# Block transposes on VectorE in the second pass's heads, an earlier K-times-values product, and reordered opening loads in a gated pooling and HGRN2 layer

## The chip, the cores and the metric

The kernel runs on one core of one Trainium2 chip. The metric is the device time of one execution in microseconds (us). A core has five engines that matter here, each with its own in-order queue: PE (TensorE: matrix products into the PSUM memory; a weight load, PEld, goes ahead of each product), DVE (VectorE), ACT (ScalarE), POOL (GpSimd) and SP (SyncE, which issues most DMAs). They meet through semaphores only.

## The reference, cut to what matters

One layer over a sequence of 2048 tokens with 1024 channels, all in float32:

```python
ada = c_act @ w_ada + b_ada                      # shift, scale, gate
h = rms_norm(x, g_pre) * (1 + scale) + shift
pv, pg, hq, hf, hi, hg, mg_pool, mg_hgrn = split(h @ w_in)
branch_a = (pool(pv) * silu(pg)) @ w_pool_o
f = lb + (1 - lb) * sigmoid(hf); k = 1 - f; q = silu(hq); v = hi
S_t = diag(f_t) S_{t-1} + k_t v_t^T;  o_t = S_t^T q_t       # per head, 8 heads of 128
branch_b = (rms_norm(o) * silu(hg)) @ w_hgrn_o
merged = sigmoid(mg_pool) * branch_a + sigmoid(mg_hgrn) * branch_b
x = x + gate * rms_norm(merged @ w_out, g_post)
```

The recurrence is computed by chunks: within a chunk the scores q times decayed k are formed and applied to v, and between chunks a 128x128 state per head is carried on.

## The kernel before, in words

Tokens are worked on in two passes (p = 0 and 1) of 1024, each in two halves (t = 0 and 1) of 512 = 4 chunks of 128. Every large product is a float32 product written as three (high and low parts, `three`, L355) and most of them are saved one in eight by a seven-product scheme (`quad`, L621). A pass has these stages: the values `V` (`v_job`, `rows7`), eight heads, the pooling projection (`a_job`), the branch-B projection (`b_fast`), and the output projection (`y_fast`).

A head h is three `quad`s: `fq` (forget gate and query), `m` (the merge gates) and `gp` (the pool part and the HGRN output gate). The last head takes `gp` before `m`. A `quad` is seven groups of 12 products of 128x512 (`pa`, `pb`, `pe` are its PSUM tiles), and after the second and each later group it calls `tick()`. A tick lets every active generator `hgrn(p, h, t)` (L676) go on to its next `yield`. Two generators (t = 0 and 1) start after each `fq`; one more tick stands after each `quad`. So a head is 21 ticks, and a generator, at about 30 yields, runs over into the next head.

What a generator does, in order: the gate F, K = 1 - F and the query Q; a tree of decay products `TT`; then scores at rising distances. For each distance it runs 16 small PE products K by Q-variants (`X`) into the PSUM tile `psa` (`scores`), DVE copies them under a mask into `PT` (`put`, L726 and L732, `COPY_PREDICATED`), and DVE multiplies K and Q by decay (`kup`, `qup`, all through L498). Five yields (`GAP`) lie between two distances. The last scores (distances 32 and 64, L801 to L807) go to `PT` by ACT (L808 to L810). After them:

- L811 and L812: `kup(32)` and `kup(64)` finish K; two yields later PE turns K's four 128x128 chunks into PSUM (`pk`, helper `turn`, L353), and ACT copies it to `KS` (L820);
- two yields later `pd` = KS times values on PE; DVE carries the state over the four chunks (`SC`, L830), starting from the tile S[h];
- three yields later `po` = PT times values plus Q times state on PE, and ACT copies the last state back to S[h] (L839);
- ACT squares and sums `po` (L843), POOL makes the norm's factor `ss`, two yields later ACT scales into `on` (L850), and two yields later PE turns `on` into PSUM (`pot`, L353); DVE multiplies it with the gate: `sgg` (L857).

In the second pass's heads every PE instruction is tied to the one written before it (`line`, `mm` L348, `turn`), so PE runs in the order of the program text. The other engines' order is set by the framework's scheduler, which places each instruction when it reckons its inputs to be there; `issue_after` (`after(...)`) adds a tie by hand.

The pool part of an even head makes window sums on DVE: `W<-PV`, `W<-W` and `pm`, with window 2 in head 0, 4 in head 2, 8 in head 4 and 16 in head 6. In an odd head it is a gate (`spg`) and needs less.

The second pass's values come from `rows7`, whose first result copies are ACT's `A.copy(vt, src)` (L1389). Weights are split into high and low part by ACT and DVE (`item_split`, `split`, L181).

The opening (first pass): SP issues `ident`, eight loads of small parameter rows (L133), eight loads of x (L515), then `w_ada` and the first weights (L384, L185). PE turns the rows (`pst`), then x (`xT`, L536), multiplies `w_ada` (L399), turns the sum (L407), and starts the values (`psV`).

Of the kernel before, what the change touches and what calls it, by code (L numbers as in the profile page):

```python
# [8 lines left out]
F32 = mybir.dt.float32  # L9
# [22 lines left out]
O_PV, O_PG, O_Q, O_F, O_I, O_G, O_MP, O_MH = 0, 512, 1024, 2048, 3072, 4096, 5120, 6144  # L32
# [36 lines left out]


@with_exitstack
def tile_block(ctx: ExitStack, tc: tile.TileContext, x, c, w_ada, b_ada, g_pre, g_post, w_in,
               pool_w, pool_scale, lb_logits, hgrn_norm_g, w_pool_o, w_hgrn_o, w_out,
               ident_d, mask_d, icnt_d, w_pv_t, x_t, w_quad, w_po, out):
    nc = tc.nc
    V, A, G, PE, SP = nc.vector, nc.scalar, nc.gpsimd, nc.tensor, nc.sync
    x, out = x[0], out[0]
    w_ada, w_in = w_ada[0], w_in[0]
# [14 lines left out]
    def utile(name, dt=F32):  # L93
        return up.tile([P, T], dt, tag="u", name=name)
# [4 lines left out]
    def after(ins):  # L99
        return tc.issue_after(ins.ins) if ins is not None else nullcontext()  # L100

    last = {"st": None, "whl": None}

    state = {"prep": 0, "use": 0, "pre": 0}

# [16 lines left out]


    ident = cst.tile([P, P], F32, name="ident")
    SP.dma_start(ident, ident_d)
    rows = utile("rows")[0:48, 0:P]
    G.memset(rows, 0.0)
    r0 = 0
    idx = {}
    for nm, src, n in (("c", c[0:1, :], 8), ("bsh", b_ada[0:1, 0:D], 8), ("bsc", b_ada[0:1, D:2 * D], 8),  # L130
                       ("gpre", g_pre[0:1, :], 8), ("lb", lb_logits[0:1, :], 8),
                       ("psc", pool_scale[0:1, :], 4), ("ng", hgrn_norm_g[0:1, :], 1)):
        SP.dma_start(rows[r0:r0 + n, :], src.rearrange("o (r k) -> (o r) k", k=P))  # L133
        idx[nm] = (r0, r0 + n)
        r0 += n
    mask = cst.tile([P, MASK_W], U8, name="mask")
# [2 lines left out]
    def const_setup():  # L139
        for o in range(0, MASK_W, T):  # L140
            w = min(T, MASK_W - o)
            mi = utile(f"mask_i{o}", I32)
            SP.dma_start(mi[:, 0:w], mask_d[:, o:o + w])
            G.tensor_copy(mask[:, o:o + w], mi[:, 0:w])
        SP.dma_start(icnt, icnt_d)

    pst = px.tile([P, T], F32, tag="px", name="pst")
    PE.transpose(pst[:, 0:48], rows, ident[0:48, 0:48])
# [31 lines left out]
    def split(src32, hi, lo, e=None):  # L180
        return A.copy(hi, src32), (e or V).tensor_tensor(lo, src32, hi.bitcast(F32), op=SUB)  # L181
# [8 lines left out]

    def item_split(name, raw):
        w = item_tile(name)
        split(raw, w[:, 0:T], w[:, T:2 * T])
        return w

    def keep(key, w, again):
# [154 lines left out]
    def turn(o, i):  # L351
        with after(line["it"] if line["on"] else None):
            line["it"] = PE.transpose(o, i, ident)  # L353
# [137 lines left out]
    def v2(ap, n):  # L491
        return ap.rearrange("p (a b) -> p a b", b=n)

    def bc(ap, n):
        return ap.unsqueeze(2).broadcast_to([P, ap.shape[1], n])

    def tt(o, a, b, op=MUL, e=None):
        return (e or V).tensor_tensor(o, a, b, op=op)  # L498
# [13 lines left out]
    def x_rows(tok, load):  # L512
        xs = [utile(f"x{tok}_{n}") for n in range(2)]
        for n in range(2):
            load(xs[n], x[tok * P:(tok + 1) * P, n * T:(n + 1) * T])  # L515
        return xs

    def x_first(cx, xss):
# [14 lines left out]
        return it, ic  # L533

    def x_turn(xss, k, tk, pt_):
        PE.transpose(pt_[:, tk * P:(tk + 1) * P], xss[tk][k // 4][:, (k % 4) * P:(k % 4 + 1) * P], ident)  # L536

    def x_turned(cx, k, pt_, on_act):
        h32 = cx["h32"][0, k] = utile(f"h32_0_0_{k}")
# [136 lines left out]
    def hgrn(p, h, t, cx):  # L676
# [104 lines left out]
        for hh in (2, 8):  # L781
            scores(X)
            put(blk(ptf, NB, hh), s48[:, :, 0:16])
            put(blk(ptf, NB, 2 * hh), s48[:, :, 16:32])
            put(blk(ptf, NB, 2 * hh), s48[:, :, 32:48])
            kup(hh)
            kup(2 * hh)
            if hh == 2:
                X = build(8, NB, 16)
            else:  # L790
                X = qp.tile([P, T], F32, tag="qr", name=f"X32_{n}")
                x32 = X[:, 0:T // 2].rearrange("p (b w) -> p b w", w=32)
                A.copy(x32, blk(Q, NB // 2, 32))
                qup(32)
                x64 = X[:, T // 2:T].rearrange("p (b w) -> p b w", w=64)
                tq = Tb[32].rearrange("p (a b) -> p a b", b=4)
                q64 = blk(Q, NT, 64)
                tt(x64, q64, bc(tq[:, :, 1], 64))
            for _ in range(GAP):
                yield  # L800
        s64 = s48  # L801
        for cc in range(NT):
# [5 lines left out]
        A.copy(pt[0:64, :, 64:128], s64[0:64, :, 32:96])  # L808
        A.copy(pt[0:32, :, 32:64], s64[0:32, :, 0:32])
        A.copy(pt[64:96, :, 96:128], s64[64:96, :, 0:32])  # L810
        kup(32)  # L811
        kup(64)  # L812
        tt(q64, x64, bc(tq[:, :, 0], 64))
        yield
        yield
        pk = px.tile([P, T], F32, tag="px", name="pk" + n)
        for cc in range(NT):
            turn(pk[:, cc * P:(cc + 1) * P], K[:, cc * P:(cc + 1) * P])
        KS = utile("KS" + n)
        A.copy(KS, pk)  # L820
        yield
        yield
        pd = px.tile([P, NT, P], F32, tag="px", name="pd" + n)
        for cc in range(NT):
            mm(pd[:, cc, :], KS[:, cc * P:(cc + 1) * P], vv(cc), True, True)
        SC = utile("SC" + n)
        sts = [S[h]]
        for cc in range(NT):
            nxt = SC[:, cc * P:(cc + 1) * P]
            V.scalar_tensor_tensor(nxt, sts[-1], Tb[128][:, cc:cc + 1], pd[:, cc, :], op0=MUL, op1=ADD)  # L830
            sts.append(nxt)
        yield
        yield
        yield
        po = px.tile([P, NT, P], F32, tag="px", name="po" + n)
        for cc in range(NT):
            mm(po[:, cc, :], pt[:, cc, :], vv(cc), True, False)
            mm(po[:, cc, :], Q[:, cc * P:(cc + 1) * P], sts[cc], False, True)
        A.copy(S[h], sts[NT])  # L839
        ss = sp.tile([P, NT], F32, tag="ss", name="ss" + n)  # L840
        for cc in range(NT):
            junk = sp.tile([P, T], BF16, tag="jx", name=f"junk{cc}_{n}", bufs=1)
# [5 lines left out]
        on = utile("on" + n)  # L848
        for cc in range(NT):
            A.activation(on[:, cc * P:(cc + 1) * P], po[:, cc, :], AF.Copy, scale=ss[:, cc:cc + 1])  # L850
        yield
        yield
        pot = px.tile([P, T], F32, tag="px", name="pot" + n)
        for cc in range(NT):
            turn(pot[:, cc * P:(cc + 1) * P], on[:, cc * P:(cc + 1) * P])
        og = cx["G"].pop((h, t))
        V.scalar_tensor_tensor(og, pot, col("ng"), og, op0=MUL, op1=MUL)  # L857
        two_out("G", p, h, t, og, cx, h == NH - 1)
# [369 lines left out]
    def krow(src, k, o):  # L1228
        return src[k * P:(k + 1) * P, o:o + T]
# [77 lines left out]
    for q in range(4):  # L1307
        parts[q] = ada_load(q)
        for k in (2 * q, 2 * q + 1)[:7 - 2 * q]:
            early["v", 0, k] = raw_load(f"e{k}", (krow(w_in, k, O_I), None))  # L1310
    xs1 = [x_rows(NT + tk, SP.dma_start) for tk in range(NT)]
    behind = {}
    ix, ic = x_first(cxs[0], xss)
    it = ada_mul(0)
    with after(ix), after(ic):
        prep()
    with after(it), after(ix):
# [46 lines left out]
    for p in range(NPASS):  # L1364
# [19 lines left out]
        if p > 0 and FAST_V:  # L1384
            def v_got(n, t, tk, src):
                vt = src
                if t == 0:
                    vt = utile(f"V{p}_{t}_{n}_{tk}")
                    A.copy(vt, src)  # L1389
# [12 lines left out]
            rows7(f"V{p}", cx["mv"], v_got, v_step)  # L1402
# [185 lines left out]
```

## Time and profile before

| | before |
|---|---|
| median of 3 runs | 1736.92 us (1736.89 to 1737.13) |
| the profiled execution | 1735.28 us |
| its span from first to last instruction | 1733.5 us |
| PE busy | 1708.2 us, 99% |
| DVE busy | 1219.8 us, 70% |
| ACT busy | 855.6 us, 49% |
| granted PE clock | 0.998 |

The 1.8 us between the profiled execution and its span lie outside of the first and last instruction. All sums are made against this one execution; the median lies 1.64 us above it, so a difference worked out in the trace is taken off the median. In a timeline a row gives start, length, engine, line, operation, output and inputs, a count, and in brackets how long the engine sat idle before, and who released it. Lengths overlap: the next instruction of an engine can begin before the one in front has ended, so the step from one start to the next is what an instruction costs in a queue.

### The profile page before, as it was taken

What the parts mean: (1) busy time and instruction counts of PE and PEld (TensorE: products, weight loads), DVE (VectorE), ACT (ScalarE), POOL (GpSimd) and SP (SyncE); (2) the same over time, 40 slices, a digit from 0 to 9 for tenths busy, and PEclk for the clock granted to TensorE, in tenths of its full rate; (3) what the DMA queues carried; (4) which work ended last, traced back from release to release, by engine and by line L of the source; (5) the groups of instructions that cost most, each with busy time, mean ns of one, the idle gap of its engine ahead of it and who ended that gap; (6) DMA issues with size and microseconds to landing.
All of it is one profiled execution on the core that took longest, in us unless ns stands there. A gap on an engine that the chain in (4) does not pass through costs nothing.

```text
span 1733.5 us, 31740 instructions
## 1 busy us (share of the span) xinstructions
PE 1708.2 (99%) x11805; PEld 1405.6 (81%) x11805; DVE 1219.8 (70%) x2546; ACT 855.6 (49%) x1975; POOL 95.9 (6%) x152
## 2 busy tenths in 40 slices
PE   7999999999999999999999999999999999999998
PEld 4788888888888887888887888888888888888886
DVE  4668888888988889788787264455455545766666
ACT  4746656566565655342755334344343343534243
POOL 1100000100000000100030000000000000000002
PEclk9999999999999999999999999999999999999999
DMA  9759887888789788976795765665665656564657
GB/s 310 270 171 331 285 305 281 294 289 324 268 290 330 265 291 283 352 252 226 268 312 173 251 203 183 203 206 173 218 194 172 218 179 193 183 231 168 210 195 265
DMA packets 191288, 425.33 MB, mean 245 GB/s; under 512 B 19311, under 2 KB 44572, under 8 KB 191134
## 3 DMA queue, kind: packets, MB, share of 16 engines
q1 hardware_dynamic: 181918, 406.52, 68.9%
q10 hardware_dynamic: 9216, 16.78, 2.7%
q8 instruction: 93, 1.52, 0.4%
q14 instruction: 61, 0.50, 0.1%
HBM read 267.51 MB, written 155.71 MB: 244 GB/s over the span
## 4 chain that ended last, share of the span: by engine, by line
PE 93%; DVE 2%; DMA 2%; ACT 2%; issue 1%; SPq 1%; POOL 0%; DVEq 0%; POOLq 0%; ACTq 0%
PE pam L348 10%; PE pagp L348 10%; PE pafq L348 10%; PE pem L348 5%; PE psA L348 5%; PE pefq L348 5%; PE psV L348 5%; PE pegp L348 5%; PE raB L348 4%; PE ray L348 4%; PE psa L348 4%; PE po L348 3%; PE pbfq L348 2%; PE pbm L348 2%; PE pbgp L348 2%; PE raV L348 2%
## 5 line engine op out<-in xcount | busy, mean ns | idle before, releaser
L181 DVE TENSOR_TENSOR whl<-wr,whl 128x512 fp32r<-128x512 f32 x160 | 108.9, 686 | 37.6 <-ACT whl L181 36.9
L181 ACT CAST whl<-wr 128x512 fp32r<-128x512 f32 x160 | 99.4, 624 | 69.1 <-issue 15.4
L348 PE MATMUL pagp<-hT,whl 128*128 128x512 f32 x384 | 128.1, 394 | 0.4 <-ACT c12gp L634 0.4
L348 PE MATMUL pam<-hT,whl 128*128 128x512 f32 x384 | 128.2, 394 | 0.2
L348 PE MATMUL pafq<-hT,whl 128*128 128x512 f32 x384 | 126.3, 390 | 0.0
L181 ACT CAST whl<-wri 128x512 fp32r<-128x512 f32 x76 | 47.1, 622 | 117.9 <-PE psA L348 27.8
L732 DVE COPY_PREDICATED PT<-mask,psa 128x256 f32<-128x256 uint8 x160 | 86.1, 547 | 11.9 <-PE psa L348 11.9
L348 PEld LDWEIGHTS pagp<-hT,whl 128*128 128x128 f32 x384 | 72.1, 188 | 16.2 <-ACT c12gp L634 0.5
L348 PEld LDWEIGHTS pam<-hT,whl 128*128 128x128 f32 x384 | 72.1, 188 | 15.4 <-ACT c12m L634 0.6
L348 PEld LDWEIGHTS pafq<-hT,whl 128*128 128x128 f32 x384 | 72.1, 188 | 15.2 <-ACT c12fq L634 0.2
L348 PE MATMUL psA<-Ph,whl 128*128 128x512 f32 x256 | 82.5, 395 | 0.4 <-ACT Ph L181 0.4
L348 PE MATMUL psV<-whl,hB 128*128 128x512 f32 x256 | 80.8, 400 | 1.6 <-ACT hB L1324 1.1
L498 DVE TENSOR_TENSOR K<-K,TT 128x256 f32<-128x256 f32 x192 | 80.6, 425 | 0.0
L348 PE MATMUL pagp<-lT,whl 128*128 128x512 f32 x192 | 74.9, 390 | 0.0
L348 PE MATMUL pam<-lT,whl 128*128 128x512 f32 x192 | 74.8, 390 | 0.0
L348 PE MATMUL pafq<-lT,whl 128*128 128x512 f32 x192 | 74.7, 389 | 0.0
L181 DVE TENSOR_TENSOR whl<-wri,whl 128x512 fp32r<-128x512 f32 x76 | 51.8, 685 | 26.1 <-ACT whl L181 25.4
L726 DVE COPY_PREDICATED PT<-mask,psa 128x256 f32<-128x256 uint8 (+1 forms) x96 | 52.1, 543 | 21.7 <-PE psa L348 21.7
L348 PEld LDWEIGHTS psa<-X,K 128*32 128x32 f32 x2816 | 48.5, 110 | 19.4 <-issue 17.1
L857 DVE SCALAR_TENSOR_TENSOR sgg<-pot,vec,sgg 128x512 f32<-128x512 f32 x32 | 23.1, 746 | 56.0 <-PE pot L353 56.0
L680 DVE TENSOR_SCALAR F<-F 128x512 f32<-128x512 f32 x16 | 6.8, 426 | 77.3 <-ACT F L679 77.2
L348 PEld LDWEIGHTS psV<-whl,hB 128*128 128x128 f32 x256 | 48.2, 191 | 14.6 <-ACT hB L181 1.7
(569 smaller groups left out, 4789.6 us busy)
## 6 DMA issues: line engine op xcount, KB each, us to landing
wr<-in_w_quad_dram SPq DMA_DIRECT2D x88, 256.0 KB, 4.0
whl<-scr_y SPq DMA_DIRECT2D x36, 512.0 KB, 3.5
sm<-Sd SPq DMA_DIRECT2D x64, 256.0 KB, 5.4
whl<-scr_b SPq DMA_DIRECT2D x32, 512.0 KB, 3.3
scr_y<-rfy SPq DMA_DIRECT2D x40, 256.0 KB, 3.1
x<-in_x_dram SPq DMA_DIRECT2D x32, 256.0 KB, 5.7
wa<-in_w_ada_dram SPq DMA_DIRECT2D x32, 256.0 KB, 6.2
V<-Vd SPq DMA_DIRECT2D x16, 512.0 KB
```

What stands on the lines that cost most here:

```text
L181: return A.copy(hi, src32), (e or V).tensor_tensor(lo, src32, hi.bitcast(F32), op=SUB)
L348: line["it"] = PE.matmul(o, lhsT=l, rhs=r, start=start, stop=stop, skip_group_check=True)
L498: return (e or V).tensor_tensor(o, a, b, op=op)
L680: V.tensor_scalar(F, F, 1e-30, None, op0=MAX)
L726: V.copy_predicated(dst.rearrange("p (c a) b -> p c a b", c=NT), m.unsqueeze(1).broadcast_to(shp), src.unsqueeze(2).broadcast_to(shp))
L732: V.copy_predicated(dst.rearrange("p (c q) a b -> p c q a b", c=NT), m, src.rearrange("p c (a b) -> p c a b", b=b).unsqueeze(2) .broadcast ...
L857: V.scalar_tensor_tensor(og, pot, col("ng"), og, op0=MUL, op1=MUL)
```

## The change

In the second pass's heads (`if p`), three things:

- K is no longer turned by PE. As soon as the second-to-last distance is done, DVE writes a decayed copy `KD` with three multiplications, and turns it into `KS` with `block_turn`: sixteen `V.transpose` instructions a generator, each over four 32x32 blocks (32 partitions x 128 elements), four in each of four ticks. The finishing `kup(32)` and `kup(64)`, PE's `pk` and ACT's copy to `KS` go, and `pd` comes right behind the last scores. Seven yields then lie ahead of `po`, where before there were two, two and three.
- The outputs `on` are turned in the same way, in the tile `ot` in SBUF, four ticks long (two in the last head), and PE's `pot` goes. The gate product reads `ot`.
- The state is handed on in `SC` (`carry`), in both passes; S[h] is copied once, at the end of pass 0.

Besides: the eight small loads become one (`rows`, packed and padded ahead of the kernel), `ident` is loaded from ACT's queue, the first `w_ada` product is tied behind the last turn of x, and in `item_split` ACT's copy of a weight is tied behind the last copy of the second pass's values (`last["act"]`).

```diff
+    def block_turn(dst, src, j):
+        d, s_ = (a.rearrange("p (c n) -> p c n", n=P) for a in (dst, src))
+        for i in range(4):
+            V.transpose(d[32 * j:32 * j + 32, :, 32 * i:32 * i + 32], s_[32 * i:32 * i + 32, :, 32 * j:32 * j + 32])
...
+                if p:
+                    KD, KS = utile("KD" + n), utile("KS" + n)
+                    tt(v2(KD, 64)[:, :, 0:32], v2(K, 64)[:, :, 0:32], bc(te(32, 1), 32))
+                    for o in (0, 32):
+                        tt(v2(KD, P)[:, :, o:o + 32], v2((KD, K)[o // 32], P)[:, :, o:o + 32], bc(te(64, 1), 32))
-            for _ in range(GAP):
+            for j in range(GAP):
+                if p and hh == 8 and j:
+                    block_turn(KS, K if j == 4 else KD, j - 1)
                 yield
...
-        kup(32)
-        kup(64)
+        if p == 0:
+            kup(32)
+            kup(64)
         tt(q64, x64, bc(tq[:, :, 0], 64))
...
-        sts = [S[h]]
+        sts = [carry.get(h, S[h])]
...
-        yield
-        yield
-        yield
+        carry[h] = sts[NT]
+        for _ in range(7 if p else 3):
+            yield
...
-        A.copy(S[h], sts[NT])
+        if t == 1 and p + 1 < NPASS:
+            A.copy(S[h], sts[NT])
+            carry[h] = S[h]
...
+        if p:
+            pot = utile("ot" + n)
+            for j in range(4):
+                if h < NH - 1 or j % 2 == 0:
+                    yield
+                block_turn(pot, on, j)
...
     def item_split(name, raw):
         w = item_tile(name)
-        split(raw, w[:, 0:T], w[:, T:2 * T])
+        with after(last["act"]):
+            A.copy(w[:, 0:T], raw)
+        V.tensor_tensor(w[:, T:2 * T], raw, w[:, 0:T].bitcast(F32), op=SUB)
...
-    SP.dma_start(ident, ident_d)
+    A.dma_start(ident, ident_d)
...
-    it = ada_mul(0)
+    with after(last["turn"]):
+        it = ada_mul(0)
```

How instructions move, at three places in the second pass's head 2 (names are pass, head and half, then a buffer number).

PE, where head 3's `fq` ends (`pafq`) and its `m` begins (`pam`); before:

```order
L348 MATMUL pafq1_3_12883<-hT41_3_10773,whl361_12933 128x512
L348 MATMUL pafq1_3_12883<-lT41_3_10774,whl361_12933 128x512
L348 MATMUL pafq1_3_12883<-hT41_3_10773,whl361_12933 128x512
L353 MATMUL pk1_2_0_13044<-ident_87,K1_2_0_12359 128x128 x4
L353 MATMUL pk1_2_1_13051<-ident_87,K1_2_1_12366 128x128 x4
L348 MATMUL pam1_3_13072<-hB111_0_9808,whl362_12949 128x512
L348 MATMUL pam1_3_13072<-lB111_0_9809,whl362_12949 128x512
```

After, the same place:

```order
L348 MATMUL pafq1_3_12978<-hT41_3_10758,whl361_13044 128x512
L348 MATMUL pafq1_3_12978<-lT41_3_10759,whl361_13044 128x512
L348 MATMUL pafq1_3_12978<-hT41_3_10758,whl361_13044 128x512
L348 MATMUL pam1_3_13193<-hB111_0_9793,whl362_13068 128x512
L348 MATMUL pam1_3_13193<-lB111_0_9794,whl362_13068 128x512
```

The eight turns of K are gone, and the two `quad`s follow each other directly; `pd`, of eight products, has moved up into the block of the last scores.

DVE, between head 2's masked copies at distance 8 and 16 and the gate F of head 3; before:

```order
L726 COPY_PREDICATED PT1_142<-mask_98,psa1_1_10925 128x16x16
L498 TENSOR_TENSOR K1_2_1_12366<-K1_2_1_12366,TT1_2_1_12431 128x16x16
L498 TENSOR_TENSOR sq1_2_1_12261<-sq1_2_1_12261,TT1_2_1_12431 128x8x32
L498 TENSOR_TENSOR X32_1_2_1_12877<-sq1_2_1_12261,TT1_2_1_12431 128x256
L680 TENSOR_SCALAR F1_3_0_12947<-F1_3_0_12947 128x512
L498 TENSOR_TENSOR c22fq1_3_12915<-pafq1_3_12883,c22fq1_3_12915 128x512
```

After:

```order
L503 TENSOR_TENSOR KD1_2_1_12963<-K1_2_1_12441,TT1_2_1_12486 128x4x32
L358 STREAM_TRANSPOSE KS1_2_0_12934<-KD1_2_0_12933 32x4x32 x4
L358 STREAM_TRANSPOSE KS1_2_1_12964<-KD1_2_1_12963 32x4x32 x4
L358 STREAM_TRANSPOSE KS1_2_0_12934<-KD1_2_0_12933 32x4x32 x4
L358 STREAM_TRANSPOSE KS1_2_1_12964<-KD1_2_1_12963 32x4x32 x4
L358 STREAM_TRANSPOSE KS1_2_0_12934<-KD1_2_0_12933 32x4x32 x4
L358 STREAM_TRANSPOSE KS1_2_1_12964<-KD1_2_1_12963 32x4x32 x4
L358 STREAM_TRANSPOSE KS1_2_0_12934<-K1_2_0_12434 32x4x32 x4
L358 STREAM_TRANSPOSE KS1_2_1_12964<-K1_2_1_12441 32x4x32 x4
L686 TENSOR_SCALAR F1_3_0_13058<-F1_3_0_13058 128x512
L503 TENSOR_TENSOR c22fq1_3_13010<-pafq1_3_12978,c22fq1_3_13010 128x512
```

All 32 turns of the head's K stand in one row on DVE, ahead of F and of `c22fq`.

DVE, where the outputs of head 1 meet the masked copies of head 2 at distance 2 and 4; before:

```order
L498 TENSOR_TENSOR sq1_2_1_12261<-X8_1_2_1_12725,TT1_2_1_12431 128x16x16
L857 SCALAR_TENSOR_TENSOR sgg1_1_0_12125<-pot1_1_0_12663,vec_102,sgg1_1_0_12125 128x512
L857 SCALAR_TENSOR_TENSOR sgg1_1_1_12088<-pot1_1_1_12670,vec_102,sgg1_1_1_12088 128x512
L732 COPY_PREDICATED PT0_141<-mask_98,psa1_0_10924 128x128x2
L498 TENSOR_TENSOR K1_2_0_12359<-K1_2_0_12359,TT1_2_0_12423 128x128x2
```

After:

```order
L503 TENSOR_TENSOR sq1_2_1_12334<-X8_1_2_1_12782,TT1_2_1_12486 128x16x16
L358 STREAM_TRANSPOSE ot1_1_0_12677<-on1_1_0_12672 32x4x32 x6
L358 STREAM_TRANSPOSE ot1_1_1_12683<-on1_1_1_12678 32x4x32 x4
L358 STREAM_TRANSPOSE ot1_1_0_12677<-on1_1_0_12672 32x4x32 x2
L358 STREAM_TRANSPOSE ot1_1_1_12683<-on1_1_1_12678 32x4x32 x4
L358 STREAM_TRANSPOSE ot1_1_0_12677<-on1_1_0_12672 32x4x32 x4
L358 STREAM_TRANSPOSE ot1_1_1_12683<-on1_1_1_12678 32x4x32 x3
L738 COPY_PREDICATED PT0_134<-mask_91,psa1_0_10909 128x128x2
L503 TENSOR_TENSOR K1_2_0_12434<-K1_2_0_12434,TT1_2_0_12478 128x128x2
```

Of the 32 turns of the outputs, 23 stand ahead of the masked copies, and nine, with the two gate products, behind them.

More of the change, by code (lines that the diff above doesn't have):

```diff
@@ L39 @@
 KINDS = (("m", "gp"), ("gp", "m"))
+ROWS = (("c", 8), ("bsh", 8), ("bsc", 8), ("gpre", 8), ("lb", 8), ("psc", 4), ("ng", 1))
 def _constants():
@@ L71, in tile_block @@
 @with_exitstack
-def tile_block(ctx: ExitStack, tc: tile.TileContext, x, c, w_ada, b_ada, g_pre, g_post, w_in,
-               pool_w, pool_scale, lb_logits, hgrn_norm_g, w_pool_o, w_hgrn_o, w_out,
-               ident_d, mask_d, icnt_d, w_pv_t, x_t, w_quad, w_po, out):
+def tile_block(ctx: ExitStack, tc: tile.TileContext, x, w_ada, b_ada, g_post, w_in, pool_w, w_pool_o, w_hgrn_o,
+               w_out, ident_d, mask_d, icnt_d, w_pv_t, x_t, w_quad, w_po, rows_d, out):
     nc = tc.nc
@@ L100, in after @@
         return tc.issue_after(ins.ins) if ins is not None else nullcontext()
-    last = {"st": None, "whl": None}
+    last = {"st": None, "whl": None, "act": None}
     state = {"prep": 0, "use": 0, "pre": 0}
@@ L124, in tile_block @@
     ident = cst.tile([P, P], F32, name="ident")
-    SP.dma_start(ident, ident_d)
+    A.dma_start(ident, ident_d)
     rows = utile("rows")[0:48, 0:P]
-    G.memset(rows, 0.0)
+    SP.dma_start(rows, rows_d)
     r0 = 0
     idx = {}
[L130 to L133, printed above, removed]
+    for nm, n in ROWS:
         idx[nm] = (r0, r0 + n)
@@ L144, in const_setup @@
             G.tensor_copy(mask[:, o:o + w], mi[:, 0:w])
-        SP.dma_start(icnt, icnt_d)
+        with after(last["x"]):
+            SP.dma_start(icnt, icnt_d)
     pst = px.tile([P, T], F32, tag="px", name="pst")
@@ L514, in x_rows @@
         for n in range(2):
-            load(xs[n], x[tok * P:(tok + 1) * P, n * T:(n + 1) * T])
+            last["x"] = load(xs[n], x[tok * P:(tok + 1) * P, n * T:(n + 1) * T])
         return xs
@@ L535, in x_turn @@
     def x_turn(xss, k, tk, pt_):
-        PE.transpose(pt_[:, tk * P:(tk + 1) * P], xss[tk][k // 4][:, (k % 4) * P:(k % 4 + 1) * P], ident)
+        last["turn"] = PE.transpose(pt_[:, tk * P:(tk + 1) * P], xss[tk][k // 4][:, (k % 4) * P:(k % 4 + 1) * P], ident)
     def x_turned(cx, k, pt_, on_act):
@@ L663, in tile_block @@
     gens = [0]
+    carry = {}
     def f_got(p, h, t, u, cx):
@@ L810, in hgrn @@
         A.copy(pt[64:96, :, 96:128], s64[64:96, :, 0:32])
-        kup(32)
-        kup(64)
+        if p == 0:
+            kup(32)
+            kup(64)
         tt(q64, x64, bc(tq[:, :, 0], 64))
-        yield
-        yield
[L816 to L820, printed above, removed]
-        yield
-        yield
+        if p == 0:
+            yield
+            yield
+            pk = px.tile([P, T], F32, tag="px", name="pk" + n)
+            for cc in range(NT):
+                turn(pk[:, cc * P:(cc + 1) * P], K[:, cc * P:(cc + 1) * P])
+            KS = utile("KS" + n)
+            A.copy(KS, pk)
+            yield
+            yield
         pd = px.tile([P, NT, P], F32, tag="px", name="pd" + n)
@@ L831, in hgrn @@
             sts.append(nxt)
-        yield
-        yield
-        yield
+        carry[h] = sts[NT]
+        for _ in range(7 if p else 3):
+            yield
         po = px.tile([P, NT, P], F32, tag="px", name="po" + n)
@@ L850, in hgrn @@
             A.activation(on[:, cc * P:(cc + 1) * P], po[:, cc, :], AF.Copy, scale=ss[:, cc:cc + 1])
[L851 to L855, printed above, removed]
+        if p:
+            pot = utile("ot" + n)
+            for j in range(4):
+                if h < NH - 1 or j % 2 == 0:
+                    yield
+                block_turn(pot, on, j)
+        else:
+            yield
+            yield
+            pot = px.tile([P, T], F32, tag="px", name="pot" + n)
+            for cc in range(NT):
+                turn(pot[:, cc * P:(cc + 1) * P], on[:, cc * P:(cc + 1) * P])
         og = cx["G"].pop((h, t))
@@ L1309, in tile_block @@
         for k in (2 * q, 2 * q + 1)[:7 - 2 * q]:
-            early["v", 0, k] = raw_load(f"e{k}", (krow(w_in, k, O_I), None))
+            with after(last["x"]):
+                early["v", 0, k] = raw_load(f"e{k}", (krow(w_in, k, O_I), None))
     xs1 = [x_rows(NT + tk, SP.dma_start) for tk in range(NT)]
@@ L1388, in v_got @@
                     vt = utile(f"V{p}_{t}_{n}_{tk}")
-                    A.copy(vt, src)
+                    last["act"] = A.copy(vt, src)
                 store("Vd", cx["Vd"][:, t * NT + tk, n * T:(n + 1) * T], vt)
@@ L1579 @@
     feed["w_po"] = np.ascontiguousarray(feed["w_pool_o"][0].reshape(4, P, KT, P).transpose(2, 1, 0, 3)).reshape(KT, P, T)
+    row_parts = [feed.pop(k)[0:1, :] for k in ("c", "g_pre", "lb_logits", "pool_scale", "hgrn_norm_g")]
+    row_parts.insert(1, feed["b_ada"][0:1, 0:2 * D])
+    flat = np.concatenate([a.ravel() for a in row_parts])
+    feed["rows"] = np.concatenate([flat, np.zeros(48 * P - flat.size, flat.dtype)]).reshape(48, P)
     for name, a in feed.items():
```

## The prediction

> **What bounds the kernel now.** I read the engines' busy time first, then the busy time by stretches of one head (in a row of it: stretch, length, PE, PEld, DVE, ACT, POOL busy with counts, PE clock, DMA share, GB/s).
>
> ```profile
> PE 1708.2 (99%) x11805; PEld 1405.6 (81%) x11805; DVE 1219.8 (70%) x2546; ACT 855.6 (49%) x1975; POOL 95.9 (6%) x152
> 1158.24:1227.43 69.19, 69.19 (x574) 57.96 (x573) 38.14 (x97) 28.98 (x77) 2.40 (x4) 1.00 0.59 191
> ```
>
> PE sets the time, and in a head of the second pass it has no idle time at all: 69.19 us busy in 69.19. What PE no longer does there is gained in full, as long as no product waits. DVE has 31 us free in a head, so it can take the turns; the question is whether they end before PE asks for them. I therefore went to the timeline, at the places where PE turns now and where DVE will.
>
> **PE's turns go.** Around K's turns (head 2's K, seen one head earlier at the same place) and the outputs' turns PE shows:
>
> ```profile
> 1124.99 0.39 PE L348 MATMUL pafq<-lT,whl 128*128 128x512 f32 x1
> 1125.22 0.39 PE L348 MATMUL pafq<-hT,whl 128*128 128x512 f32 x1
> 1126.56 0.40 PE L348 MATMUL pam<-lB,whl 128*128 128x512 f32 x1
> 1157.04 0.40 PE L348 MATMUL pegp<-hT,whl 128*128 128x512 f32 x1
> 1157.27 1.03 PE L353 MATMUL pot<-ident,on 128*128 128x128 f32 x8
> 1158.24 0.89 PE L348 MATMUL psa<-X,K 128*32 128x48 f32 x64
> 1172.59 0.39 PE L348 MATMUL pagp<-hT,whl 128*128 128x512 f32 x1
> 1172.90 0.89 PE L348 MATMUL psa<-X,K 128*32 128x48 f32 x64
> ```
>
> From the last `pafq` to the second `pam` are 1.34 us (1125.22 to 1126.56); without turns between them it would be two steps of 0.23 (1124.99 to 1125.22), so K's eight turns cost 0.88. From the last `pegp` to the scores behind the outputs' turns are 1.20 us; where scores follow a product directly it is 0.31 (1172.59 to 1172.90): 0.89. Eight heads at 1.77 are 14.2 us off PE. `pd` only moves, at the same cost. ACT's copies to `KS` and S go; ACT isn't late in the heads, so that counts as nothing.
>
> **What the turns meet on DVE.** Let t be DVE's step from one block turn to the next. A head gets 64 of them and six products for `KD`. DVE works in order, and there are two gaps to fill.
>
> ```profile
> 1153.03 1.92 ACT L850 ACTIVATE on<-po,ss 128x128 f32<-128x128 f32 x7
> 1157.91 1.41 DVE L857 SCALAR_TENSOR_TENSOR sgg<-pot,vec,sgg 128x512 f32<-128x512 f32 x2 [7.00 <-PE pot L353]
> 1090.05 0.72 DVE L732 COPY_PREDICATED PT<-mask,psa 128x256 f32<-128x256 uint8 x1
> 1093.50 0.42 DVE L732 COPY_PREDICATED PT<-mask,psa 128x256 f32<-128x256 uint8 x1
> 1165.47 0.71 DVE L498 TENSOR_TENSOR W<-PV 128x527 f32<-128x527 f32 x1 [2.37 <-ACT PV L867]
> 1178.81 0.42 DVE L498 TENSOR_TENSOR X<-sq,TT 128x256 f32<-128x256 f32 x1
> 1186.41 0.43 DVE L680 TENSOR_SCALAR F<-F 128x512 f32<-128x512 f32 x1 [7.18 <-ACT F L679]
> 1048.07 0.43 DVE L680 TENSOR_SCALAR F<-F 128x512 f32<-128x512 f32 x1 [7.96 <-ACT F L679]
> 1117.29 0.43 DVE L680 TENSOR_SCALAR F<-F 128x512 f32<-128x512 f32 x1 [8.80 <-ACT F L679]
> 1463.16 0.43 DVE L680 TENSOR_SCALAR F<-F 128x512 f32<-128x512 f32 x1 [5.96 <-ACT F L679]
> 1187.54 0.22 PE L348 MATMUL psa<-X,K 128*32 128x32 f32 x1
> 1165.50:1180.00 14.50, 14.50 (x125) 11.80 (x125) 11.54 (x24) 4.11 (x10) 0.00 (x0) 1.00 0.55 183
> 1442.30:1457.20 14.90, 14.90 (x127) 12.15 (x126) 13.90 (x28) 4.15 (x10) 0.00 (x0) 1.00 0.55 178
> 1096.30:1108.50 12.20, 12.20 (x115) 9.91 (x114) 8.99 (x18) 2.43 (x4) 0.00 (x0) 1.00 0.66 215
> 1522.46 0.43 DVE L726 COPY_PREDICATED PT<-mask,psa 128x256 f32<-128x256 uint8 x1
> ```
>
> The first gap is the 7.00 us in which DVE waits for `pot`. Outputs are in `on` from about 1153.9 (middle of the seven scalings), so turns can start 4 us before the gate products did. The second is the 6 to 9 us ahead of F. In head 2 the chain on DVE runs: 1153.9; 23 turns; ten masked copies and K products, 3.9 (1090.05 to 1093.93, the same place in the head before); nine turns and two gate products of together 1.3; from `W` to the end of `X` 13.7 (1165.47 to 1179.2) less the 2.1 idle in it, 11.7; `KD`, 1.5; 32 turns. The end is 1172.3 + 64t. It can't come before 1179.8 + 32t, since the `X` work waits for PE's scores (1179.2 less the 0.9 gained on PE, plus `KD`). Who waits: the first `pd`, due half of the last scores (0.76) behind their start at 1187.54, 0.9 earlier by the gone turns, when all but four turns must be done; so the whole is due at about 1188.5. Behind the turns F and `c22fq` are queued, and the next `quad` waits for its PSUM tile through `c22fq`; that wait falls into the same stall of PE.
>
> The other heads differ by the pool's sums, in DVE's busy time of the same stretch: 11.54 in head 2, 13.90 in head 6, and I put head 4 midway. That gives 1173.4 + 64t in head 4 and 1174.6 + 64t in head 6 in the same frame. In odd heads the stretch is shorter (8.99): 1100.4 + 64t, not before 1109.1 + 32t, against 1119.4 (one period of 69.18 before 1188.5, all rounded). Head 0 turns no outputs ahead of K: 1041.6 + 32t against 1051.1. Head 7 is the roughest: from its last masked copies at 1522.46 come 0.33, `KD` and some 4.3 of the projections' work that DVE does there, 1528.6 + 32t, against an estimated 1534.5. The stalls, summed over eight heads: 0.8 us at t = 0.20; 2.3 at 0.23; 5 at 0.25; 12.6 at 0.285 (heads 2, 4, 6, 7 with 2.0, 3.1, 4.3, 3.2); 26 at 0.32, where the odd heads begin to wait too.
>
> **What a turn costs.** No row has this operation, so the nearest ones bound it.
>
> ```profile
> 1066.12 0.28 DVE L498 TENSOR_TENSOR TT<-TT 128x128 f32<-128x128 f32 x1
> 1066.32 0.34 DVE L830 SCALAR_TENSOR_TENSOR SC<-SC,TT,pd 128x128 f32<-128x128 f32 x1
> L498 DVE TENSOR_TENSOR TT<-TT 128x128 f32<-128x128 f32 x32 | 8.9, 285 | 0.1
> L498 DVE TENSOR_TENSOR sm<-sm,sm 128x512 f32<-128x512 f32 x40 | 27.0, 684 | 0.1
> 7.25 0.17 DVE L163 TENSOR_TENSOR small<-small 128x8 f32<-128x8 f32 x1
> 7.46 0.17 DVE L164 TENSOR_TENSOR small<-small 128x8 f32<-128x8 f32 x1
> ```
>
> A turn passes 128 elements a lane. Low end: operations of 128 elements that don't wait for each other step by 0.20 (1066.12 to 1066.32). They take 1.04 ns an element (684 less 285 over 384), so 0.133 and a fixed 0.067; `KD`'s products, two of 256 elements and four of 128, are then 2 x 0.333 + 4 x 0.20 = 1.5. I take 0.23 for the turn, the low row plus 0.033 for the 32 columns that must be in before a block can leave; that surcharge is a guess, and the choice is the low row because the turns write apart from each other. High end: an operation that needs the one before it starts 0.04 after its end (7.25 + 0.17 to 7.46). With the 0.285 that 128 elements last, and the block's 0.033, that makes t some 0.32 to 0.35. Less than 0.20 is excluded by the elements that must pass.
>
> The Trainium skill, "VectorE: DVE Perf Modes", § The three transpose paths, gives 311 ns for a VectorE transpose of 128x128 in bfloat16. Taken as t, an estimate by that page, the stalls would be some 21 us and the whole about 3 us slower, near 1740; the sum here goes by the rows instead.
>
> **The opening.**
>
> ```profile
> 0.72 0.39 SPq L125 DMA_DIRECT2D ident<-in_ident_dram  x1
> 3.55 3.67 SPq L515 DMA_DIRECT2D x<-in_x_dram  x8
> 7.26 6.63 DMA wa<-in_w_ada_dram
> 23.28 3.34 PE L348 MATMUL psV<-whl,hB 128*128 128x512 f32 x8 [1.14 <-ACT hB L1324]
> ```
>
> SP issues `ident` at 0.72 and comes to x at 3.55; with one rows load, that would be at about 1.1, and w_ada, the weights and `psV` behind it could all move up by 2.4. I take 2.3. The bounds are 0, if the bytes of w_ada (6.63 us to land) or the norm's work on x hold `psV` at 23.28, and 3. SP is passed by nothing else; `ident` leaves ACT's queue at its head. The later tie of the `w_ada` product behind x's turns costs nothing while the weights land later than x.
>
> **The second pass's values.**
>
> ```profile
> 920.74 0.73 PE L348 MATMUL rxV1T<-whl,hT 128*128 128x512 f32 x2 [1.75 <-ACT V L1389]
> 918.38 1.30 ACT L181 CAST whl<-wri 128x512 fp32r<-128x512 f32 x2 [2.58 <-issue]
> 920.11 2.04 ACT L1389 COPY V<-rxV1B 128x512 f32<-128x512 f32 x4
> ```
>
> PE waits 1.75 us for ACT's value copies, which stood behind two weight casts that themselves waited 2.58 us. Now the casts are tied behind the copies: 1.6 gained, with 0 and 1.75 as bounds. What is queued behind the tied casts is ACT's later work; `whl` is wanted by the first head, and four copies take only 2.04 us, so I count no loss.
>
> **The sum.** 14.2 + 2.3 + 1.6 = 18.1 us off, less the stalls. At t = 0.23: 15.8 off, 1735.28 to 1719.5 in the profiled execution, 1721.1 on the median, which lies 1.64 above it; I say 1721.0. The sign turns where the stalls reach 18.1, at t = 0.303.
>
> **The rivals.** *First: every turn waits until the one before it has ended.* A turn starts on another 32-partition block than its predecessor each time, and no row of the profile has two such operations in a row, so nothing speaks against it but that independent operations do overlap (0.20). Then t lies at 0.285 to 0.345; it decides above 0.303. At 0.32 the stalls are 25.8, the net is 7.7 slower, 1744.6; at 0.345 about 36, which is 18 slower, near 1755; at 0.285 still 5.5 faster. I give it 0.35: 0.03 of it faster, 0.10 the same, 0.22 slower.
>
> The Trainium skill, "VectorE: DVE Perf Modes", § Two Vector instructions with no wait between them, has a rule of this sort: an instruction whose first input or whose output starts in another 32-partition quarter than the previous one's is held until every earlier Vector instruction has finished. By that rule this rival would come about; no run here shows it yet.
>
> *Second: the turns go as forecast, but the opening and the value copies give nothing*, because `psV` is held by the bytes of w_ada and by x rather than by the issue, and PE's wait at 920.74 moves to the casts. Then 14.2 less 2.3 stalls, 11.9 off: 1725.0. For it speaks that `psV` waits for ACT's hB and not for a DMA. I give it 0.10, all faster.
>
> **How the numbers follow.** The forecast, t from 0.20 to 0.25, has 0.50, all faster, and its own range is 1717 (t = 0.20 with the larger gains) to 1726 (t = 0.25 and half of the small gains). With the rivals' 0.35 and 0.10, 0.05 is left for what I don't see, mostly on PE's ordered row (0.02 same, 0.03 slower). Faster by over 0.2%: 0.50 + 0.10 + 0.03 = 0.63; within 0.2% (3.5 us, about what a measurement of this kernel can tell from no change): 0.12; slower: 0.25. The range reaches from 1716 over both gains to 1748, a little above the first rival's 1744.6; a t of 0.345 and more is left out.
>
> **What would show it.** In the changed kernel's timeline: the step of the block turns on DVE, which decides all (0.23, against 0.30 and above). PE's waits for `KS` ahead of `pd`, none in odd heads, below 1 us in head 6; F and `c22fq` starting before PE needs them. The step from `pafq` to `pam`, 0.23 where it was 1.34 over two. `psV` starting near 21, x issued near 1.1. No wait of PE at `rxV1T`. Wrong it would be if PE shows waits of 2 us and more in every even head, if DVE's step is above 0.30, or if the gate products, now on the far side of nine turns, hold up the branch-B projection.

## The result and the profile after

The changed kernel takes 1769.18 us (median of 4 runs, 1766.92 to 1771.09) against 1736.91 before: 1.0187 times as long, interval 1.0175 to 1.0199. The forecast was 1721.0, its range 1716 to 1748. Its profiled execution has a span of 1769.3 us, 35.8 more than before.

The engines' busy time after:

```profile
PE 1713.3 (97%) x11677; PEld 1401.7 (79%) x11677; DVE 1376.2 (78%) x3074; ACT 845.8 (48%) x1935; POOL 98.1 (6%) x151
```

PE has 128 instructions less and is busy 5 us longer; DVE is busy 156 us longer for 512 turns and, `KD` less `kup`, 16 products more. Before, PE had next to no waits in the heads. After, the longest groups of PE's waits (who waited for whom: total, times, longest one) are these; waits of the opening stand between them:

```profile
PE pagp L348 <- DVE c22gp L503: 17.3, 6, 3.0
...
PE pd L348 <- DVE KS L358: 6.6, 5, 2.3
PE rxB1B L348 <- DVE lB11g L179: 3.9, 1, 3.9
PE pam L348 <- DVE c22m L503: 3.3, 1, 3.3
```

That is 31.1 us of waits, and the largest is not the one ahead of `pd` on which the prediction's sum rests. It is for `c22gp`, in heads 1 to 6. DVE's timeline of head 2 shows how it comes about:

```profile
1153.58 7.24 DVE L358 STREAM_TRANSPOSE ot<-on 32x128 f32<-32x128 f32 x23 [3.04 <-ACT on L867]
...
1164.74 1.92 DVE L358 STREAM_TRANSPOSE ot<-on 32x128 f32<-32x128 f32 x6
1166.68 0.75 DVE L881 SCALAR_TENSOR_TENSOR sgg<-ot,vec,sgg 128x512 f32<-128x512 f32 x1
...
1171.20 0.68 DVE L503 TENSOR_TENSOR c22gp<-pagp,c22gp 128x512 f32<-128x512 f32 x1
...
1178.15 0.44 DVE L738 COPY_PREDICATED PT<-mask,psa 128x256 f32<-128x256 uint8 x1 [1.41 <-PE psa L348]
...
1184.90 7.56 DVE L358 STREAM_TRANSPOSE KS<-KD 32x128 f32<-32x128 f32 x24
1192.47 2.55 DVE L358 STREAM_TRANSPOSE KS<-K 32x128 f32<-32x128 f32 x8
1195.06 0.43 DVE L686 TENSOR_SCALAR F<-F 128x512 f32<-128x512 f32 x1
```

The turns start at 1153.58, close to the 1153.9 of the prediction, and step by 0.316 (23 in 7.24, 24 in 7.56). In the row, each turn starts about 0.014 us after the one before it has ended (it lasts 0.30). All 32, the masked copies and the gate products stand in DVE's queue ahead of `c22gp`, which starts at 1171.20 where before it was:

```profile
1167.57 0.69 DVE L498 TENSOR_TENSOR c22gp<-pagp,c22gp 128x512 f32<-128x512 f32 x1
```

What PE does in the meantime:

```profile
1171.94 0.79 PE L348 MATMUL pagp<-hT,whl 128*128 128x512 f32 x1 [2.96 <-DVE c22gp L503]
1172.54 0.63 PE L348 MATMUL pagp<-lT,whl 128*128 128x512 f32 x1
1172.96 1.05 PE L348 MATMUL pagp<-hT,whl 128*128 128x512 f32 x2
...
1178.35 0.50 PE L348 MATMUL pafq<-hB,whl 128*128 128x512 f32 x1
...
1193.79 1.16 PE L348 MATMUL pd<-V,KS 128*128 128x128 f32 x8 [0.72 <-DVE KS L358]
```

PE waits 2.96 us, and then its products step by 0.42 (1172.54 to 1172.96) where 0.23 is usual. The busy times by two-microsecond stretches around the same wait of head 1 say why; the column behind POOL is the granted clock:

```profile
1098.00:1100.00 2.00, 0.40 (x1) 0.40 (x2) 1.55 (x3) 0.42 (x1) 0.00 (x0) 0.82 0.97 299
1100.00:1102.00 2.00, 2.00 (x6) 1.52 (x6) 1.29 (x2) 0.64 (x2) 0.00 (x0) 0.50 0.84 283
1102.00:1104.00 2.00, 2.00 (x12) 1.34 (x10) 1.45 (x2) 0.20 (x1) 0.00 (x0) 0.83 0.67 270
```

Behind the wait PE runs at half its clock, which is why it is busy longer with less to do. The clock record of this trace has 0.50 for 3.41 us here (1099.27 to 1102.68), and for 3.41 or 6.83 us at each of the eight waits of 2.8 to 3.9 us. The Trainium skill, "TensorE: Matmul & The Clock Gate", § What's actually happening, describes this: a window without work puts the array to half rate, and it takes a busy window to release it. The trace agrees with the half rate (0.50); the page's idle window is about 3.4 us, while here waits of 2.80 us already did it.

Over the span the mean granted clock is 0.988, in the kernel without turns below 0.998 at a span of 1733.2. That is 1.2% of 1769.3 less 0.2% of 1733.2, about 18 us. So against that kernel: 14.2 us of PE's turns gained, 31.1 of waits and 18 of clock lost, 34.7 of the 36.1 us between the two profiled spans. This is the bookkeeping of one execution, the longest of the four. The other three have clocks of 0.991 to 0.993, by the same working 5 to 9 us less of clock lost, and spans only 1.4 to 4.2 us shorter; the terms are not independent prices.

### The profile page after: what moved, and what is told of

Same layout as the page of the kernel before. It is cut to its first block, busy times and chain, and to the rows that moved or that the text cites. A ratio compares the mean times of both kernels' runs of the same rounds, so it can differ in the third digit from the quotient of the medians.

```text
span 1769.3 us, 31969 instructions
## 1 busy us (share of the span) xinstructions
PE 1713.3 (97%) x11677; PEld 1401.7 (79%) x11677; DVE 1376.2 (78%) x3074; ACT 845.8 (48%) x1935; POOL 98.1 (6%) x151
## 4 chain that ended last, share of the span: by engine, by line
PE 81%; DVE 14%; issue 2%; ACT 2%; DMA 2%; SPq 0%; POOL 0%; DVEq 0%; ACTq 0%; POOLq 0%
PE pam L348 9%; PE pagp L348 9%; PE pafq L348 8%; PE pem L348 5%; PE psV L348 5%; PE pefq L348 4%; PE psA L348 4%; PE pegp L348 4%; PE raB L348 3%; PE psa L348 3%; PE ray L348 3%; PE po L348 3%; DVE KS L358 2%; PE pbm L348 2%; PE pbfq L348 2%; PE raV L348 2%
## 5 line engine op out<-in xcount | busy, mean ns | idle before, releaser
L348 PE MATMUL pagp<-hT,whl 128*128 128x512 f32 x384 | 137.6, 421 | 17.7 <-DVE c22gp L503 17.3
L348 PEld LDWEIGHTS pagp<-hT,whl 128*128 128x128 f32 x384 | 77.5, 202 | 38.0 <-DVE c22gp L503 19.9
L358 DVE STREAM_TRANSPOSE ot<-on 32x128 f32<-32x128 f32 x256 | 77.5, 303 | 20.5 <-ACT on L867 16.8
L348 PE MATMUL pagp<-lT,whl 128*128 128x512 f32 x192 | 79.4, 414 | 0.0
L503 DVE TENSOR_TENSOR K<-K,TT 128x256 f32<-128x256 f32 x160 | 67.4, 423 | 0.0
L348 PE MATMUL psa<-X,K 128*32 128x48 f32 (+2 forms) x2816 | 60.2, 210 | 0.2 <-DVE PT L732 0.2
L358 DVE STREAM_TRANSPOSE KS<-KD 32x128 f32<-32x128 f32 x192 | 57.9, 302 | 2.5
```

What stands on the lines that cost most here:

```text
L348: line["it"] = PE.matmul(o, lhsT=l, rhs=r, start=start, stop=stop, skip_group_check=True)
L358: V.transpose(d[32 * j:32 * j + 32, :, 32 * i:32 * i + 32], s_[32 * i:32 * i + 32, :, 32 * j:32 * j + 32])
```

## The experiments

The theory after the first look: the turns are as slow as in the prediction's first rival (0.316), because each starts in another quarter of the partitions; and the loss sits mostly with the outputs' turns, ahead of `c22gp`. Against it stood the prediction's own sum (the loss sits with K's turns, ahead of `pd`), and a turn that takes 0.30 by itself.

**K's turns alone.** Outputs turned by PE:

```diff
-        if p:
+        if False:
             pot = utile("ot" + n)
```

> Only K is turned on VectorE, the outputs by PE as before; all else as in the change. Theory (most of the loss comes from the outputs' turns, which stand ahead of c22gp on DVE): no wait of PE for c22gp and no slow clock behind it; in the before kernel's gaps K's 32 turns at 0.316 cause waits ahead of pd of about 8 us in all, against 7 us of PE turns and 3 us of opening gained: about 1735, within 4 us of before. Rival (the loss sits with K's turns ahead of pd, as the prediction's sum had it): 1755 or more.

1739.98 us, 1.0019 (1.0009 to 1.0028). PE's waits for `KS` are the only long ones in the heads:

```profile
PE pd L348 <- DVE KS L358: 7.4, 5, 2.3
```

5 us above the expectation, and far below the rival's: against the kernel without turns (below) K's turns cost 7.1 us, though PE does 7 us less.

**The outputs' turns alone.** K turned by PE as before (`pk`, its copy, `kup(32)` and `kup(64)`):

```diff
-            for j in range(GAP):
-                if p and hh == 8 and j:
-                    block_turn(KS, K if j == 4 else KD, j - 1)
+            for j in range(GAP):
                 yield
...
-        if p == 0:
+        if True:
             yield
             yield
             pk = px.tile([P, T], F32, tag="px", name="pk" + n)
```

> Only the outputs are turned on VectorE, K by PE as before; all else as in the change. Theory: PE's waits for c22gp (17 us), the slow clock behind them (about 14 us), the wait in head 7 and for lB11g at the end (11 us) all stay, 7 and 3 us are gained: about 1769, as slow as the change. Rival (K's turns carry the loss): 1735 or less.

1763.27 us, 1.0150 (1.0135 to 1.0166), 6 us below the expectation. Its waits:

```profile
PE pagp L348 <- DVE c22gp L503: 17.3, 6, 3.0
...
PE pam L348 <- DVE c22m L503: 3.3, 1, 3.3
PE rxB1B L348 <- DVE lB11g L179: 3.2, 1, 3.2
```

The outputs carry four fifths of the loss: against the kernel without turns (next) they add 30.4 us, K's turns 7.1. Together 37.5, and the change adds 36.3, so the two nearly add up. The slow clock does not follow each of these waits: behind three of the eight PE goes on at full clock, its products 0.23 apart, as here in head 3:

```profile
1249.37 0.50 PE L348 MATMUL pagp<-hT,whl 128*128 128x512 f32 x1 [2.81 <-DVE c22gp L503]
1249.71 0.39 PE L348 MATMUL pagp<-lT,whl 128*128 128x512 f32 x1
1249.94 0.63 PE L348 MATMUL pagp<-hT,whl 128*128 128x512 f32 x2
```

**No turns at all.** Both edits above:

> No turn on VectorE at all: the opening, the tie of the weight casts behind the value copies and the state handed on are left. Both theories: the 3.0 us that the changed kernel was ahead at the start of the second pass's heads, and PE busy in the heads as before: 1733.9. If the opening and the copies give nothing by the end: 1737.

1732.85 us, 0.9981 (0.9973 to 0.9990): 3.7 us faster than its own runs of before, 0.7 more than expected.

**Turns that stay in one quarter.** Each block's source comes from the quarter that it is written to, so the output holds other data:

```diff
-            V.transpose(d[32 * j:32 * j + 32, :, 32 * i:32 * i + 32], s_[32 * i:32 * i + 32, :, 32 * j:32 * j + 32])
+            V.transpose(d[32 * j:32 * j + 32, :, 32 * i:32 * i + 32], s_[32 * j:32 * j + 32, :, 32 * j:32 * j + 32])
```

> The changed kernel, with each block turn's source taken from the quarter of partitions that it writes to (so off-diagonal blocks hold other data and the output is not the reference's); as many turns, of the same size. Four turns in a row then start in the same quarters. If the step of 0.316 comes from the change of quarter: about 0.20 to 0.23 within a group, no waits for c22gp, and about 1722. If a turn takes 0.30 by itself, whatever its neighbours: the step stays at 0.316 and the time at 1769.

1725.93 us, 0.9936 (0.9923 to 0.9950). K's turns of head 1 on DVE:

```profile
1108.64 4.97 DVE L358 STREAM_TRANSPOSE KS<-KD 32x128 f32<-32x128 f32 x24
1113.62 1.68 DVE L358 STREAM_TRANSPOSE KS<-K 32x128 f32<-32x128 f32 x8
```

24 turns in 4.98 us are 0.21 each. Eight turns in a row (four of each half) now keep their quarters; within such a group they step by 0.19, each starting 0.06 us before the one ahead has ended, and only the turn that begins a new group waits for that end. The step of 0.316 therefore does not belong to the operation, and with it the waits for `c22gp` are gone. One rival is left open by this run: each of its turns also reads and writes the same quarter. The run with pairs, below, settles that. The Trainium skill, "VectorE: DVE Perf Modes", § Two Vector instructions with no wait between them, states that an instruction which starts in another quarter is held until all earlier ones have finished; the trace agrees: 0.014 us behind the end in the change, 0.06 ahead of it here.

**Work in PE's wait.** Twelve products at the place of the wait for `c22gp`, into a tile that nobody reads:

```diff
         got(0, 1, u2)
         tick()
+        if ...:  # heads 1 to 6 of the second pass, gp
+            junk = px.tile([P, T], F32, tag="px", name="junk" + name)
+            for _ in range(12):
+                mm(junk, mv["T4", 0][0][:, 0:P], mv["T4", 0][0], True, True)
         prod(a, "T4", False)
```

> The changed kernel with twelve added products in heads 1 to 6, at the place on PE where it waits for c22gp (2.7 us of work, written to a PSUM tile that nobody reads). Theory (behind a wait of 2.9 us PE runs at half its clock for 3 us and more, which doubles the price of the wait): the added work lies inside the wait, the products behind it step by 0.23 instead of 0.43, and the kernel gets 14 us faster although PE does more: about 1755. Rival (the slow products are not a consequence of PE's idling, but of DVE's or the DMAs' work at that time): 1769 or more.

1768.93 us, 1.0186 (1.0171 to 1.0201): no gain that can be told, where 14 us were expected. PE in head 2:

```profile
1168.80 2.88 PE L348 MATMUL junkgp<-hT 128*128 128x512 f32 x12
1171.92 0.50 PE L348 MATMUL pagp<-hT,whl 128*128 128x512 f32 x1 [0.24 <-DVE c22gp L503]
...
1175.73 0.50 PE L348 MATMUL pafq<-hB,whl 128*128 128x512 f32 x1
...
1192.52 1.16 PE L348 MATMUL pd<-V,KS 128*128 128x128 f32 x8 [2.08 <-DVE KS L358]
1194.87 2.08 PE L348 MATMUL pd<-V,KS 128*128 128x128 f32 x8
1196.60 0.77 PE L348 MATMUL pefq<-hB,whl 128*128 128x512 f32 x1
```

Half of the theory holds, and the rival's reason is refuted though its time came true: with PE kept busy, the products behind the wait run at full clock (`pafq` at 1175.73, 2.6 us earlier than in the change, though this execution began head 1 1.4 us later: 4.0 gained). The other half falls: PE then waits longer for `KS` (2.08 us instead of 0.72), the clock drops there (the second `pd` takes 2.08 instead of 1.16), and `pefq` starts at 1196.60 (1196.61 in the change), so that 2.6 of the 4.0 are given back. Head 6 gives back more, with a wait of 4.17 instead of 2.25 and a slow clock behind it:

```profile
1484.69 2.07 PE L348 MATMUL pd<-V,KS 128*128 128x128 f32 x8 [4.17 <-DVE KS L358]
```

All waits for `KS` add up to 11.3 us instead of 6.6. In an even head DVE's row from the outputs' turns to the last turn of K sets the pace; much of what PE saves in between it waits for at the end. The slow clock is a full price only where DVE's row is not behind it.

**Turns of the two halves in pairs.** The second generator issues both halves' turns, alternating, so that every second turn keeps its quarters:

```diff
+        both = (first.pop((key, j)), ds)
         for i in range(4):
-            V.transpose(d[32 * j:32 * j + 32, :, 32 * i:32 * i + 32], s_[32 * i:32 * i + 32, :, 32 * j:32 * j + 32])
+            for d, s_ in both:
+                V.transpose(d[32 * j:32 * j + 32, :, 32 * i:32 * i + 32], s_[32 * i:32 * i + 32, :, 32 * j:32 * j + 32])
```

> The changed kernel, with the turns of the two halves alternating one by one, so that each second turn starts in the same quarters as the one before it; the outputs' gate product comes one tick later. Theory (a change of quarter costs 0.1 us, and PE's price at c22gp more than doubles by the clock): a mean step of 0.26; each set of 32 turns ends 1.9 us sooner; the wait for c22gp falls from 2.9 to about 1.0 us, too short for the slow clock; the waits for KS fall below 2 us in all: about 1731. If the step stays 0.316: 1769.

1750.19 us, 1.0080 (1.0065 to 1.0095): 19 us better than the change, 19 short of what was expected. DVE and PE in head 2:

```profile
1153.80 6.63 DVE L365 STREAM_TRANSPOSE ot<-on 32x128 f32<-32x128 f32 x23 [3.03 <-ACT on L874]
```

```profile
1170.91 0.50 PE L348 MATMUL pagp<-hT,whl 128*128 128x512 f32 x1 [1.71 <-DVE c22gp L510]
1171.25 0.40 PE L348 MATMUL pagp<-lT,whl 128*128 128x512 f32 x1
1171.48 0.62 PE L348 MATMUL pagp<-hT,whl 128*128 128x512 f32 x2
```

The outputs' first turns are not paired, since the first half's outputs are ready before the second's; 23 take 6.63 instead of 7.24. The wait falls to 1.71, where about 1.0 was expected, and behind it the clock stays up (0.23 a step); over six heads 9.7 us of it are left. The waits for `KS` stay at 6.6 us in all, as if the last experiment's account held here too: what PE saves earlier it waits for there.

The pairs also settle the rival that the run in one quarter left open. In three pairs of four the second turn moves its data from one quarter to another just as the first does, yet it starts 0.235 us after the first, which lasts 0.30; the next pair's first turn starts 0.014 us after the end of the second. So what costs is the change of quarter from one turn to the next, not the move within a turn.

**The outputs earlier.** Three yields ahead of `po` instead of seven:

```diff
-        for _ in range(7 if p else 3):
+        for _ in range(3):
```

> The changed kernel with three yields instead of seven ahead of po, so that the outputs and their turns come four ticks (some 13 us) earlier, where DVE has idle time around c22m, and no longer stand ahead of c22gp. Theory (the place of the outputs' turns carries the loss, not their number or step): no wait for c22gp and none for lB11g, the waits for KS as with K's turns alone (7 us), 7 us of PE's output turns gained on that kernel: about 1733. Rival (the 20 us that the turns add to DVE in a head are too many wherever they stand): a new wait, for c22m or for the first scores' copies, and 1750 or more.

1743.57 us, 1.0036 (1.0024 to 1.0049). With as many turns at the same step it is 26 us faster than the change: neither `c22gp` nor `lB11g` is waited for. Still it is 10 us above the expectation. Its longest waits in the heads:

```profile
PE pd L348 <- DVE KS L358: 7.0, 5, 2.2
...
PE pagp L348 <- ACT pbgp L644: 4.4, 6, 0.7
PE pam L348 <- DMA whl<-scr_('m', 7)_6_7999: 3.3, 1, 3.3
```

ACT's copy `pbgp` is late by 0.7 in each of six heads, and in head 7 a weight load is. Neither was in the expectation; the waits for `KS` were.

**Both.** Pairs, and outputs early:

> Both: three yields ahead of po, and the turns of the two halves alternating. Theory: no wait for c22gp, waits for KS below 2 us: about 1727, faster than the kernel before and than the kernel without turns (1733). Rival (DVE too full): 1745 or more.

1727.46 us, 0.9948 (0.9934 to 0.9963), as expected, though 3.0 us of waits for `KS` are left where less than 2 were expected. On DVE and in PE's waits:

```profile
1105.15 6.09 DVE L365 STREAM_TRANSPOSE KS<-KD 32x128 f32<-32x128 f32 x24
```

```profile
PE pd L348 <- DVE KS L365: 3.0, 3, 1.3
```

24 paired turns last 6.09 us, 0.254 each, the mean of 0.316 and 0.19.

**The opening alone.** The kernel without turns, and without the tie of the casts:

```diff
-        with after(last["act"]):
-            A.copy(w[:, 0:T], raw)
-        V.tensor_tensor(w[:, T:2 * T], raw, w[:, 0:T].bitcast(F32), op=SUB)
+        split(raw, w[:, 0:T], w[:, T:2 * T])
```

> No turn on VectorE and no tie of the weight casts behind the value copies: of the change only the opening (and the state handed on) is left. If the 2.5 us that the first product starts earlier last to the end: 1734.2. If they are given back in the first pass's projections, as the traces with and without turns suggest (the lead there falls from 2.4 to between 1.5 and -1.3 us): 1736 or more. The kernel without turns, with the tie, took 1732.9; the tie would then be worth the rest.

1734.13 us, 0.9984 (0.9975 to 0.9993): by the median 2.4 us are gained, about the 2.5 that the first product starts earlier. Its profiled span (1733.8, before 1733.5) shows no gain, but that execution is the slowest of its eleven and the one of before is faster than its median. The interval reaches from 1.2 to 4.3 us, so how much stays is left open. The tie would be worth the 1.3 us to the kernel without turns, which the two overlapping intervals don't tell from nothing.

**K's product later.** K's turns on DVE, outputs by PE, `pd` two yields later and `po` where it was:

```diff
+        for _ in range(2 if p else 0):
+            yield
         pd = px.tile([P, NT, P], F32, tag="px", name="pd" + n)
...
-        for _ in range(7 if p else 3):
+        for _ in range(5 if p else 3):
```

> K's turns on VectorE, the outputs by PE, and the product of K and values two ticks later (as far behind the last scores as PE's turns of K stood before), po at the same place. Theory (what K's turns cost is only the early place of pd; DVE has the time): the waits for KS (7.4 us) go, what is late next is c22fq behind the turns, below 2 us in all: about 1727. Rival (DVE's chain holds the heads whatever PE waits for): a wait for c22fq or for the first scores of about the same size, 1735 or more.

1728.99 us, 0.9955 (0.9942 to 0.9969): 11 us better than with `pd` right behind the scores. What is late next is `c22fq`, and little:

```profile
PE pafq L348 <- DVE c22fq L503: 0.8, 2, 0.5
```

**All three.** Pairs, `pd` one yield later, two yields from there to `po`:

> The paired turns with outputs early (1727.5), with pd one tick later behind the last scores. Theory: its waits for KS (3.0 us) go: about 1724.5. Rival: the wait moves to c22fq, 1727.

1723.12 us, 0.9922 (0.9908 to 0.9935): faster than the kernel before by 13 us, and the fastest kernel here. Two heads of it on PE, and the waits for `KS`:

```profile
1167.23 0.50 PE L348 MATMUL pafq<-hB,whl 128*128 128x512 f32 x1
...
1234.62 0.50 PE L348 MATMUL pafq<-hB,whl 128*128 128x512 f32 x1
```

```profile
PE pd L348 <- DVE KS L365: 1.0, 1, 1.0
```

A head takes 67.39 us instead of 69.19: 1.80 less.

## Why the prediction was wrong

- **What bounds the kernel** was right, and so was the gain on PE. 1.77 a head was forecast, and a head without waits is 1.80 shorter.
- **The step of a turn** failed: "I take 0.23 for the turn". It is 0.316, next to the 0.32 at which the first rival was priced, and for the reason that the rival gave. The argument for 0.23 was that the turns write apart from each other; what counts here is that each of four turns reads from another quarter than the one before. (Nor is 0.20 a floor: turns that stay in their quarters step by 0.19.) By the prediction's own formula 0.316 gives about 24 us of stalls and 1743 us, still within the range.
- **The places where PE waits** failed, and that put the result out of the range. The sum took only `pd` as a place that the turns can make late, and of `c22fq` said that its wait "falls into the same stall of PE". `c22gp`, which stands behind all 32 turns of the outputs, was not in it at all, though it is one of the 0.69 us operations in the busy time of the stretch 1165.50 to 1180.00 that the sum used. At 0.23 the outputs' turns would have ended 2.8 us sooner (32 times 0.086), about when PE needs `c22gp`; at 0.316 it is the largest wait: 17.3 us. At `pd`, where the formula has 24, PE waited 6.6, since it comes there late itself (with the added products, when it comes earlier, 11.3). The same was missed in head 7 (`c22m`, 3.3) and behind it in the branch-B projection (`lB11g`, 3.9), which the prediction names among its signs of being wrong but does not price.
- **"less the 2.1 idle in it"** was wrong too: in head 2 DVE's row is idle for 0.70 and 0.69 us between its own operations, through ACT, and 1.41 us for PE's slowed scores, before it comes to K. These 2.8 us don't vanish when DVE is late.
- **Small slips in the working**, on which nothing turns: the stalls at 0.20 come out at 0.5 by its own terms, not 0.8; the lower end 1717 is taken off the profiled execution, off the median it is 1719. The opening had seven small row loads, not eight.
- **The slow clock** was no term of the sum: about 18 us of the span. The filler shows that in the even heads much of it is hidden behind DVE's row, and how often it comes differs from execution to execution (granted clocks of 0.988 to 0.993).
- **The opening and the value copies** came as forecast in the trace. x is issued at 1.17 (about 1.1 forecast), the first product of the values starts 2.46 us earlier than at 23.28 (2.3 forecast), and no wait at `rxV1T` is left. For both 3.9 were forecast, 3.7 measured without turns; how much of it is the opening's is open, as said. In the changed kernel's timeline:

```profile
20.82 2.12 PE L348 MATMUL psV<-whl,hB 128*128 128x512 f32 x8 [1.14 <-ACT hB L1350]
```

- **The sign** had a chance of 0.25. The first rival was the mechanism, but priced at `pd` alone.

## What to carry to other kernels

When work moves to another engine, list for that engine every operation that its partners wait for, not only the one that uses the moved result, and check each against the moved row at the pessimistic step; here the loss sat at an operation that has nothing to do with the turns but stands behind them. When such a row holds a partner, saving time in the partner gives little until the row itself is shortened or moved to where the engine idles. Both together turned the same edit from 32 us slower into 13 us faster.

## What the hardware showed that was not expected

- A VectorE turn of four 32x32 blocks steps by 0.19 us when it starts in the same quarters of partitions as its predecessor, and by 0.316 when it doesn't, since it then starts 0.014 us behind the other's end; alternating two sources brings 0.254.
- A wait of PE can be followed by 3.41 or 6.83 us at half the granted clock, so it can cost about double its length (2.96 us of wait and 2.9 of slower work in head 2). The length of the wait alone does not decide: in the run without turns 1.74 us did it, in the run with the added products 3.27 us did not. In each trace's clock record the stretches between two changes are whole multiples of 3.41 us (68.27 is twenty of them). So where a wait lies against these steps may decide; no run here tests that.
